# Operand tiles at 0, 32, 64 or 96 bytes into their buffers, and a smaller reserved ring

## The chip, the cores and the metric

One core of a Trainium2 chip runs the whole program. The metric is the device time of one execution in microseconds. The engines named below are TensorE (PE in the rows; PEld is its loading of weights), VectorE (DVE), ScalarE (ACT), GpSimd (POOL) and SyncE (SP), which issues the DMAs.

## What is computed

Two blocks of two layers each on 512 tokens of 1024 features, in float32. What matters of the reference:

```python
# first block, per layer
h = h + 0.5 * (1.0 + gt1) * swiglu(hn, w_ffn1_in[l], w_ffn1_out[l])     # d_ff 2816
mixed = jnp.concatenate([y_att, y_rwkv, y_conv], axis=-1) @ w_mix_out[l]
h = h + (1.0 + gt2) * mixed
h = h + 0.5 * (1.0 + gt3) * swiglu(hn, w_ffn2_in[l], w_ffn2_out[l])
# second block, per layer: the stream x and a context of 256 tokens
out_x, out_c = token_mixers(hx, hc, ...)                                # mLSTM, Fourier, convolution
x = x + mx[2] * rmsnorm(out_x, g_post_mix[l])
x = x + mx[5] * rmsnorm(sq_relu_mlp(hx, w_mlp1[l], w_mlp2[l]), g_post_mlp[l])   # hidden 4096
```

`hn`, `hx` and `hc` are normed and modulated activations. Nearly all of the arithmetic is in the dense products (`@`).

## The kernel before, in words

Activations lie feature-major in SBUF: eight blocks of 128 features, each a tile of 128 partitions by 512 tokens (the context: 256). A dense product takes its weights in panels of 128 output features (128 x 1024 numbers). Both operands are split into a high and a low part in the type float32r, and a product is three passes.

**loadw** (L376) brings one panel by DMA from SP into a raw buffer (two of them), ScalarE casts it to `wh` (L387), VectorE subtracts to give `wl` (L388). There are four buffers for `wh`, four for `wl`, and extra pools where a group of panels has more than four.

**mm3_steps** (L395) is the product of one panel with the eight (or seven, or four) blocks of an operand. For each block it issues three matmuls, and each loads its own 128 x 128 weights:

```python
nc.tensor.matmul(ps, wl[:, s], xh[:, sl], start=k == 0, stop=False)     # L401
nc.tensor.matmul(ps, wh[:, s], xl[:, sl], start=False, stop=False)      # L402
nc.tensor.matmul(ps, wh[:, s], xh[:, sl], start=False, stop=k == n - 1) # L403
```

**sweep** runs panels over segments: the panels in the middle of a phase over all 512 tokens at once, those at its head and tail over halves of 256 tokens, so that the next phase can begin on one half. The operands are `xn` (the normed activations, written by Norm at L275 and L276 or in the opening), `hid` (the hidden panels of an FFN or MLP, written through `split`, L454 and L455), and `xh`/`xl`, `ch`/`cl` and `xr` (mixed outputs, most of them through `split_new`). The order of the work is the program's own; TensorE executes in that order.

**Where the tiles lie.** A pool's buffers follow one another in each partition, each rounded up to 32 bytes. In front stand the reserved ring for dynamic DMAs (16,384 bytes) and four constants (128), then the pool `one`: 544 (onesP), 512 (ident), 8 x 2048 (h), 32, 32, 2496 (cols), 2048 and 1024 (acc). The raw buffers then begin at byte 39,584, which is 309 x 128 + 32. Raw, `wh` and `wl` buffers are 4096 bytes each and the blocks of an operand 2048 (the context: 1024), so that all buffers of a pool have the same remainder modulo 128:

| tiles | first byte | remainder modulo 128 |
|---|---|---|
| `wh`, `wl` (the pools of four) | 47,776 and 64,160 | 32 |
| `xn`, `xh`, `xl`, `xr` of the stream | 92,576 | 32 |
| `hid` of the FFNs (first block) | 128,960 | 64 |
| `wh`, `wl` of the extra pool at the tail of an FFN | 190,400 | 64 |
| `xn`, `ch`, `cl` of the context | 135,648 | 96 |
| `hid` of the MLPs (second block) | 176,608 | 96 |

The slices of a panel for single matmuls are 512 bytes apart, the halves of a block 1024, so a slice has the remainder of its tile.

Of the kernel before, what the change touches and what calls it, by code (L numbers as in the profile page):

```python
"""Two-layer macaron hybrid block followed by a two-layer joint block with a context stream.

Activations live on chip feature-major ([feature, token]); every dense product runs on the tensor
engine in float32r with both operands split exactly into a high and a low part (three passes).
"""
# [8 lines left out]
F32 = mybir.dt.float32  # L14
F32R = mybir.dt.float32r
# [8 lines left out]
T = 512  # L24
# [29 lines left out]
# order of the query heads: block j holds heads j and 4 + j, so that each shares its partitions  # L54
# with the key/value head it attends to
# [18 lines left out]
def _pack(i):  # L74
# [55 lines left out]
    feat = np.r_[2048 + 16:2832, 0:1024, 1024:2048]      # F, C | q, k | v, o  # L130
# [16 lines left out]
def _consts():  # L147
# [5 lines left out]
    c1[:, CI_G1:CI_G1 + 64] = s <= t                     # columns of R  # L153
    c1[:, CI_G1 + 64:CI_G1 + 128] = s < t                # columns of A
# [19 lines left out]
    def dft(n):  # L174
        """cos for frequencies up to n / 2 + 1, then -sin for those below n / 2."""
        j = np.arange(n)
        an = 2 * np.pi * (j[:, None] * j[None] % n) / n
        half = np.concatenate([np.cos(an[:, :n // 2 + 2]), -np.sin(an[:, :n // 2])], axis=1) / math.sqrt(n)
        return np.ascontiguousarray(half.reshape(n // 128, 128, n + 2).astype(f))
# [10 lines left out]

HA, HB = slice(0, 256), slice(256, 512)
OPEN = 5            # panels that go along with the first norm, block by block
GRP = 4             # panels at the head of a phase that go segment by segment
HLAST = 6           # the same in the last MLP
FTAIL = 7           # panels at the tail of an FFN that go segment by segment
MTAIL = 8           # the same of a token mixing
MORE = 3            # temporaries of their own for its tail
DEEP = 2            # hidden panels that go segment by segment with the whole last product of an MLP
DMORE = 3           # temporaries of their own there
PAIR = 4            # squares added up on VectorE  # L200
OFIRST = 3          # output gates ahead of the recurrence
YORD = (6, 7, 0, 1, 2, 3, 4, 5)      # order in which the mixed features become ready
ATT_EVERY = 0.8     # steps per round of what runs side by side
# [5 lines left out]
class MeanSq:  # L209
    """Mean squares over the features of a stream, token-major in PSUM, part by part. The squares of the  # L210
    eight blocks are added up on VectorE, four at a time, and then on the tensor engine (in the one group
    that the zeros open), or on VectorE alone (n: tokens of the stream)."""
# [41 lines left out]
class Norm:  # L254
    """Norm and modulation of a stream, part by part, into split operand tiles."""
# [7 lines left out]
    def __call__(self, acc, sl):  # L263
        k, nc = self.k, self.k.nc
        if self.X is None:
            new = lambda: self.pool.tile([128, self.n], F32R, name="xn", tag=self.tag)
            self.X = [(new(), new()) for _ in range(8)]
# [11 lines left out]
class Kernel:  # L279
    def __init__(self, ctx, tc, a):  # L280
# [4 lines left out]
        self.turn = 0  # L285
# [26 lines left out]
    def temp(self, n, name):  # L312
        """Short-lived [128, n]; half-width ones have buffers of their own."""
        if n > 256:
            return self.tmp.tile([128, T], F32, name=name, tag="nt")[:, :n]
        if self.more is not None and name != "nt":
            return self.more[0].tile([128, 256], F32, name=name, tag=name, bufs=self.more[1])[:, :n]
        return self.tmp.tile([128, 256], F32, name=name, tag="n2", bufs=3)[:, :n]

# [1 line left out]
    def cond_rows(self, pool, i, after=None):  # L321
        """silu of condition i on every partition; not before the tile `after` is there (its use in a
        busy stretch would only delay others)."""
# [10 lines left out]
    def ada_piece(self, pool, src, b0, key, j0, cbs, names):  # L334
        """8 output blocks: one column tile [128, 8] for each conditioning vector in cbs. The work is
        queued in steps; spare() emits them."""
# [16 lines left out]
    def spare(self, n=None):  # L353
        """Emits n queued steps, or all."""
# [20 lines left out]
    def loadw(self, src, pool=None):  # L375
        """src: a weight panel, or several that share a tile."""  # L376
# [8 lines left out]
        wh = (pool or self.whp).tile([128, 1024], F32R, name="wh", tag="wh")  # L385
        wl = (pool or self.wlp).tile([128, 1024], F32R, name="wl", tag="wl")
# [19 lines left out]
    def sweep(self, panels, segs, consume, head=0, tail=0, done=None, extra=None):  # L406
        """panels: weight panels (DRAM); segs: (key, X, slice) in the order in which they become ready.
        The first `head` and the last `tail` panels go segment by segment. consume(panel, key, slice,
        psum); done(key, slice) after a segment's last. extra: room for the weights of groups of over four.
        Narrow panels are loaded in pairs."""  # L410
# [16 lines left out]
        for gi, (ps_, sg) in enumerate(groups):  # L427
# [5 lines left out]
            for key, X, sl in sg:  # L433
                for c in range(0, len(ps_), side):
                    # side by side, block by block as the operand becomes ready
# [21 lines left out]
    def split_new(self, pool, src, tag, n=T, **k):  # L457
        hi = pool.tile([128, n], F32R, name=tag + "h", tag=tag, **k)
        lo = pool.tile([128, n], F32R, name=tag + "l", tag=tag, **k)
# [4 lines left out]
    def scratch(self, name):  # L464
        """Small columns; a phase that runs beside another takes its own."""
# [4 lines left out]
    def rsqrt(self, v):  # L470
        """1/sqrt(v) of v [128, n] (positive): the exponent guess (within 3.5%), a step with fitted
        constants (6.6e-4) and one of third order (1e-9)."""
# [5 lines left out]
        # y holds 3/8 of the root from here on  # L478
# [9 lines left out]
    def stat(self, srcs, sel, n, pp):  # L488
        """Sums over features of srcs * sel: PSUM [128 tokens, tile, w]."""
# [10 lines left out]
    def spread(self, rs, n, w, pp, wp=None, wb=2):  # L500
        """rs [128 tokens, tile, w] -> PSUM [128 features in w groups, n tokens]."""
# [31 lines left out]
    def sigmoid(self, dst, src, bias=0.0):  # L533
        """dst = sigmoid(src + 2 bias) = (1 + tanh(src / 2 + bias)) / 2."""
# [5 lines left out]
    def ffn(self, l, which, norm, gt, nxt, ada=()):  # L540
        """h += 0.5 (1 + gt) swiglu(norm(h)); nxt() gives the norm that follows; norm None: the opening."""
        nc, tc, a = self.nc, self.tc, self.a
        wi, wo = a[f"f{which}i"][l], a[f"f{which}o"][l]
        with ExitStack() as st:
# [7 lines left out]
            for pi, kc in enumerate(pieces):  # L552
                last = pi == len(pieces) - 1
                hid = [tuple(hp.tile([128, T], F32R, name="hid", tag="hid") for _ in range(2)) for _ in range(kc)]
# [43 lines left out]
    def opening(self, hp, adap, panels, up):  # L598
        """The first norm and the first panels, block by block as the input comes in."""
# [3 lines left out]
        with ExitStack() as st:  # L603
# [40 lines left out]
            def block(j):  # L644
# [3 lines left out]
                hi, lo = (self.xp.tile([128, T], F32R, name="xn", tag="x") for _ in range(2))  # L648
# [23 lines left out]
    def attention(self, l, ap, qkv, Z):  # L672
        """A generator. qkv: projected tiles q0-q3, k, v; the outputs, split, go to Z."""
# [12 lines left out]
        # key norm, with the query's gain folded in  # L686
# [6 lines left out]
        # values, token-major  # L693
# [61 lines left out]
        for j in range(4):  # L755
# [3 lines left out]
            # query scales per (token, head): rs * 64 ** -0.5  # L759
# [36 lines left out]
    def shift(self, l, dst, ps, j, sl, last):  # L796
        """Token shift of projected block j out of PSUM; last [128, 1] carries the column before."""
# [11 lines left out]
    def rwkv_group(self, l, rp, P, p, hf):  # L809
        """A pair of heads over half of the tokens; P: shifted projections r0 r1 k0 k1 v0 v1 wdad gd,  # L810
        whose tiles take what comes of them. A generator, so that two pairs can be emitted side by side;
        it returns the output."""
# [16 lines left out]
        # decay and its running sums per chunk  # L829
# [16 lines left out]
        # normalised removal key  # L846
# [20 lines left out]
        # bonus (in v) and gate (in r)  # L867
# [12 lines left out]
        # group norm, bonus, gate  # L880
# [14 lines left out]
    def rwkv_chunks(self, rp, p, RAV, BKB, ep, yp):  # L895
        """Four chunks of 64 tokens for a pair of heads; head 1 has its chunk rows on partitions 64-127."""
# [6 lines left out]
        # for each head and chunk: columns of R, of A, [B K] token-major, [A V] token-major; the rows of  # L903
        # head 1 have their halves the other way round
# [18 lines left out]
        for n in range(6):  # L923
# [17 lines left out]
            if n < 5:  # L941
                # so far nothing lies outside the diagonal blocks of 32
                nc.vector.transpose(Tm.rearrange("p i t -> p (i t)"), TT.rearrange("p i t -> p (i t)"))
            yield
        # M2 V
# [47 lines left out]
    def mesh(parts):  # L993
        """Generators side by side: (generator, its steps per round)."""
# [17 lines left out]
    def mix1(self, l, norm, gt, nxt):  # L1012
# [7 lines left out]
        with ExitStack() as st:  # L1020
# [70 lines left out]
            def rest():  # L1091
                """The rows of w_mix_out of the recurrence and the convolution."""
# [3 lines left out]
                rs = [tuple(self.xp.tile([128, T], F32R, name="xr", tag="x") for _ in range(2)) for _ in range(2)]  # L1096
# [48 lines left out]
    def gates(self, mp, ps, bias, n, m0, gM):  # L1145
        """Running sums and maxima of the gates; rows 0-3 forward, 64-67 backward. A generator that returns them."""
# [25 lines left out]
        gc = mp.tile([128, nt, 4, 4], F32, name=tag, tag=tag)      # g_f, -m_f, g_b, -m_b  # L1172
# [7 lines left out]
    def rows_spread(self, mp, src, name):  # L1180
        """src [128, 1] with rows 0-3 and 64-67 -> [128, 2, 4] on every partition."""
# [34 lines left out]
    def mlstm_head(self, mp, hd, q, k, V1, M, gt, state, sig, gcol, n):  # L1216
        """One head of a stream; sig (sigmoid of the output gate) becomes the mixed output. A generator."""
# [465 lines left out]
```

## Time and profile before

| | before |
|---|---|
| median of 2 runs | 3742.06 us (3741.11 to 3743.01) |
| span of the profiled execution | 3742.2 us |
| TensorE busy | 3674.9 us |
| VectorE busy | 2297.0 us |
| ScalarE busy | 1365.2 us |
| matmuls | 21700 |

A row of the timeline gives the start of an instruction, its duration, its engine, line, operation, the tiles written and read, and shapes. The end of a matmul is modelled, and matmuls overlap in the pipeline: the difference between two starts is the time that one takes of the engine. A row of the groups gives count, busy time and the mean duration of one.

### The profile page before, as it was taken

The page shows a single profiled execution, that of the slowest core. Times are in us where ns is not written, and L with a number is a line of the kernel's source. Part 1 is how long each engine was busy: PE and PEld are TensorE (multiplying, and loading weights), DVE is VectorE, ACT ScalarE, POOL GpSimd, SP SyncE. Part 2 cuts the span into 40 slices and gives each one's busy share as a digit, 9 for nine tenths or more (in the row PEclk, how much of TensorE's full clock was granted, in tenths as well). Part 3 has the DMA queues.
Part 4 walks back from the last instruction along what each step waited for, and adds up shares of the span by engine and source line. Part 5 has one row for each costly group of instructions (what it writes and reads, how often), then busy time and mean ns, then how long its engine had stood idle before and what let it go on. Part 6 is the DMA issues. An engine that isn't in the chain of part 4 may idle for free.

```text
span 3742.2 us, 54388 instructions
## 1 busy us (share of the span) xinstructions
PE 3674.9 (98%) x21700; PEld 3127.7 (84%) x21700; DVE 2297.0 (61%) x4858; ACT 1365.2 (36%) x2505; POOL 5.7 (0%) x42
## 2 busy tenths in 40 slices
PE   8999999999999999999999999999999999999998
PEld 6888877988898889778888888899888897888887
DVE  7565656653356545575778599675644469864334
ACT  3222444422232224443322343455223244354332
POOL 0000000000000000000000000000000000000000
PEclk9999999999999999999999999999999999999999
DMA  7565200263336543111555311123434311132332
GB/s 264 189 208 163 82 29 29 90 215 120 99 97 208 181 138 96 46 36 68 161 191 184 109 53 40 34 81 113 146 113 130 107 36 57 49 94 84 97 96 73
DMA packets 123727, 412.24 MB, mean 110 GB/s; under 512 B 13873, under 2 KB 17713, under 8 KB 123474
## 3 DMA queue, kind: packets, MB, share of 16 engines
q1 hardware_dynamic: 123474, 408.77, 33.8%
q8 instruction: 170, 2.79, 0.3%
q14 instruction: 83, 0.68, 0.1%
HBM read 406.56 MB, written 2.10 MB: 109 GB/s over the span
## 4 chain that ended last, share of the span: by engine, by line
PE 93%; DVE 5%; ACT 1%; DMA 1%; issue 1%; SPq 0%; DVEq 0%; ACTq 0%
PE mm L401 23%; PE mm L402 22%; PE mm L403 22%; PE mc L401 2%; PE mc L403 2%; PE mc L402 2%; PE my L402 2%; PE my L401 2%; PE my L403 2%; PE pn L1268 1%; PE stat L497 1%; PE spr L512 1%; PE sc L712 1%; PE pS L1252 1%; PE po L750 1%
## 5 line engine op out<-in xcount | busy, mean ns | idle before, releaser
L401 PE MATMUL mm<-xn,wl 128*128 128x512 f32 (+1 forms) x2680 | 1011.6, 378 | 3.6 <-DVE rst L483 2.5
L402 PE MATMUL mm<-xn,wh 128*128 128x512 f32 (+1 forms) x2680 | 1004.5, 375 | 0.0
L403 PE MATMUL mm<-xn,wh 128*128 128x512 f32 (+1 forms) x2680 | 1000.0, 373 | 0.0
L388 DVE TENSOR_TENSOR wl<-raw,wh 128x1024 fp32r<-128x1024 f32 (+3 forms) x538 | 636.9, 1185 | 466.1 <-ACT wh L387 464.5
L387 ACT CAST wh<-raw 128x1024 fp32r<-128x1024 f32 (+3 forms) x538 | 546.4, 1017 | 940.2 <-PE mm L403 429.1
L401 PEld LDWEIGHTS mm<-xn,wl 128*128 128x128 f32 x2680 | 507.4, 189 | 97.0 <-issue 12.4
L403 PEld LDWEIGHTS mm<-xn,wh 128*128 128x128 f32 x2680 | 507.2, 189 | 88.0 <-issue 2.1
L402 PEld LDWEIGHTS mm<-xn,wh 128*128 128x128 f32 x2680 | 507.5, 189 | 86.1 <-issue 5.2
L401 PE MATMUL mm<-hid,wl 128*128 128x512 f32 (+1 forms) x1250 | 455.2, 364 | 2.1 <-DVE ox L1587 1.9
L403 PE MATMUL mm<-hid,wh 128*128 128x512 f32 (+1 forms) x1250 | 455.5, 365 | 0.0
L402 PE MATMUL mm<-hid,wh 128*128 128x512 f32 (+1 forms) x1250 | 454.3, 364 | 0.0
L345 DVE CUSTOM_DVE_ANT_0 adaj<-adar,cb 128x1024 bf16<-128x1024 f32 x288 | 351.6, 1221 | 18.5 <-DMA adar<-in_ada_dram 11.0
L401 PEld LDWEIGHTS mm<-hid,wl 128*128 128x128 f32 x1250 | 234.8, 188 | 41.2 <-DVE ox L1587 2.3
L403 PEld LDWEIGHTS mm<-hid,wh 128*128 128x128 f32 x1250 | 234.8, 188 | 40.2
L402 PEld LDWEIGHTS mm<-hid,wh 128*128 128x128 f32 x1250 | 234.7, 188 | 40.1
L565 DVE TENSOR_TENSOR sg<-sg,mm 128x512 f32<-128x512 f32 (+1 forms) x80 | 53.4, 667 | 187.9 <-PE mm L403 182.3
L561 ACT ACTIVATE sg<-mm 128x512 f32<-128x512 f32 (+1 forms) x85 | 49.5, 582 | 301.4 <-PE mm L403 301.4
L402 PE MATMUL mc<-xn,wh 128*128 128x256 f32 x512 | 145.6, 284 | 0.0
L401 PE MATMUL mc<-xn,wl 128*128 128x256 f32 x512 | 145.5, 285 | 0.0
L403 PE MATMUL mc<-xn,wh 128*128 128x256 f32 x512 | 144.6, 283 | 0.0
L401 PE MATMUL mm<-xh,wl 128*128 128x256 f32 x448 | 129.7, 290 | 5.0 <-ACT xh L454 2.9
L402 PE MATMUL mm<-xl,wh 128*128 128x256 f32 x448 | 128.3, 286 | 0.5 <-DVE xl L455 0.5
(432 smaller groups left out, 5325.6 us busy)
## 6 DMA issues: line engine op xcount, KB each, us to landing
adar<-in_ada_dram SPq DMA_DIRECT2D x240, 512.0 KB, 4.5
raw<-in_m_dram SPq DMA_DIRECT2D x96, 512.0 KB, 3.6
raw<-in_f1i_dram SPq DMA_DIRECT2D x88, 512.0 KB, 3.5
raw<-in_f2i_dram SPq DMA_DIRECT2D x88, 512.0 KB, 3.6
raw<-in_w2i_dram SPq DMA_DIRECT2D x46, 512.0 KB, 3.5
raw<-in_mixi_dram SPq DMA_DIRECT2D x40, 512.0 KB, 3.4
raw<-in_m_dram SPq DMA_DIRECT2D x64, 256.0 KB, 3.0
raw<-in_f1o_dram SPq DMA_DIRECT2D x32, 448.0 KB, 3.4
```

The lines of the kernel that those rows point to most:

```text
L345: nc.vector.tensor_tensor_reduce(junk, raw, cb, 1.0, 0.0, ALU.mult, ALU.add, ot[:, j:j + 1])
L387: nc.scalar.copy(wh[:, :n], raw[:, :n])
L388: nc.vector.tensor_sub(wl[:, :n], raw[:, :n], wh[:, :n].bitcast(F32))
L401: nc.tensor.matmul(ps, wl[:, s], xh[:, sl], start=k == 0, stop=False)
L402: nc.tensor.matmul(ps, wh[:, s], xl[:, sl], start=False, stop=False)
L403: nc.tensor.matmul(ps, wh[:, s], xh[:, sl], start=False, stop=k == n - 1)
L497: nc.tensor.matmul(ps[:, j, :], s[:, j * 128:(j + 1) * 128], sel, start=k == 0, stop=k == len(srcs) - 1)
L512: nc.tensor.matmul(ps[:, j * 128:(j + 1) * 128], lhs, self.ident, start=True, stop=True)
L561: nc.scalar.activation(sg, ps, AF.Silu)
L565: nc.vector.tensor_mul(sg, sg, ps)
L712: nc.tensor.matmul(ps[:, i, (0 if qt else 128):], q[rows, qt * 128:(qt + 1) * 128], kn[rows, k0:(qt + 1) * 128], start=True, stop=True)
L750: nc.tensor.matmul(po[rows, qt * 128:(qt + 1) * 128], vt[:, qt - 1 + b, rows], ptt[:, i, b, :], start=n_ == 0, stop=n_ == len(bs) - 1)
```

## The change

Operand tiles get 32 numbers (128 bytes) of room more, and the slice that is used begins 0, 32, 64 or 96 bytes into the buffer. For `xn` and `hid` the place goes by the number of the block, for `wh` and `wl` by a running number of the panel, for `split_new` and `xr` it is always 0. The high and the low part of a block or a panel have the same place. The reserved ring for dynamic DMAs is 1 KB. Comments and docstrings are blanked out, so that lines keep nearly their numbers.

```diff
+PADW = 32
...
-            new = lambda: self.pool.tile([128, self.n], F32R, name="xn", tag=self.tag)
-            self.X = [(new(), new()) for _ in range(8)]
+            new = lambda j: self.k.offset(self.pool, "xn", self.tag, self.n, j)
+            self.X = [(new(j), new(j)) for j in range(8)]
...
-        self.turn = 0
+        self.turn = self.panel = 0
...
+    def offset(self, pool, name, tag, n, j, **k):
+
+        o = 8 * (j % 4)
+        return pool.tile([128, n + PADW], F32R, name=name, tag=tag, **k)[:, o:o + n]
+
...
-        wh = (pool or self.whp).tile([128, 1024], F32R, name="wh", tag="wh")
-        wl = (pool or self.wlp).tile([128, 1024], F32R, name="wl", tag="wl")
+        self.panel += 1
+        wh = self.offset(pool or self.whp, "wh", "wh", 1024, self.panel)
+        wl = self.offset(pool or self.wlp, "wl", "wl", 1024, self.panel)
...
-        hi = pool.tile([128, n], F32R, name=tag + "h", tag=tag, **k)
-        lo = pool.tile([128, n], F32R, name=tag + "l", tag=tag, **k)
+        hi = self.offset(pool, tag + "h", tag, n, 0, **k)
+        lo = self.offset(pool, tag + "l", tag, n, 0, **k)
...
-                hid = [tuple(hp.tile([128, T], F32R, name="hid", tag="hid") for _ in range(2)) for _ in range(kc)]
+                hid = [tuple(self.offset(hp, "hid", "hid", T, j) for _ in range(2)) for j in range(kc)]
...
-                hi, lo = (self.xp.tile([128, T], F32R, name="xn", tag="x") for _ in range(2))
+                hi, lo = (self.offset(self.xp, "xn", "x", T, j) for _ in range(2))
...
-                rs = [tuple(self.xp.tile([128, T], F32R, name="xr", tag="x") for _ in range(2)) for _ in range(2)]
+                rs = [tuple(self.offset(self.xp, "xr", "x", T, 0) for _ in range(2)) for _ in range(2)]
...
-                hid = {k: [tuple(hp.tile([128, n], F32R, name="hid", tag=f"hid{k}") for _ in range(2)) for _ in range(kc)]
+                hid = {k: [tuple(self.offset(hp, "hid", f"hid{k}", n, j) for _ in range(2)) for j in range(kc)]
...
-    nc = _bacc.Bacc("TRN2", target_bir_lowering=False, num_devices=1)
+    nc = _bacc.Bacc("TRN2", target_bir_lowering=False, num_devices=1, dynamic_dma_scratch_size=1024)
```

## Rows read from the trace of the kernel before

**Rows 1.** The page: busy time, share and instructions; granted clock in 40 slices.

```profile
PE 3674.9 (98%) x21700; PEld 3127.7 (84%) x21700; DVE 2297.0 (61%) x4858; ACT 1365.2 (36%) x2505; POOL 5.7 (0%) x42
...
PEclk9999999999999999999999999999999999999999
```

**Rows 2.** The page: the chain that ended last, shares of the span by engine.

```profile
PE 93%; DVE 5%; ACT 1%; DMA 1%; issue 1%; SPq 0%; DVEq 0%; ACTq 0%
```

**Rows 3.** Groups by shape, whole span: count, busy us, mean ns, idle before.

```profile
L401 PE MATMUL mm<-xn,wl 128*128 128x512 f32 x2200 | 874.3, 397 | 0.8 <-ACT yx L1384 0.6 <-ACT sg L561 0.2
...
L401 PE MATMUL mc<-xn,wl 128*128 128x256 f32 x512 | 145.5, 285 | 0.0
...
L401 PE MATMUL mm<-xh,wl 128*128 128x256 f32 x448 | 129.7, 290 | 5.0 <-ACT xh L454 2.9 <-DVE h L1084 1.7 <-DVE wl L388 0.4
```

**Rows 4.** Groups by shape in the first block (0 to 2177 us).

```profile
L401 PE MATMUL mm<-hid,wl 128*128 128x512 f32 x478 | 188.9, 395 | 0.0
```

**Rows 5.** Groups by shape in the second block (2177 us to the end).

```profile
L401 PE MATMUL mm<-hid,wl 128*128 128x512 f32 x448 | 175.2, 391 | 0.0
```

**Rows 6.** Timeline over xn: start us, duration us, instruction; one load of weights.

```profile
999.69 0.39 PE L401 MATMUL mm<-xn,wl 128*128 128x512 f32 x1
...
1000.15 0.19 PEld L401 LDWEIGHTS mm<-xn,wl 128*128 128x128 f32 x1
...
1007.85 0.39 PE L401 MATMUL mm<-xn,wl 128*128 128x512 f32 x1
```

**Rows 7.** Timeline of TensorE over the hid of an FFN, 512 columns.

```profile
839.68 0.40 PE L401 MATMUL mm<-hid,wl 128*128 128x512 f32 x1
...
845.51 0.39 PE L402 MATMUL mm<-hid,wh 128*128 128x512 f32 x1
```

**Rows 8.** Timeline over the MLP's hid: 512 columns, then the context's 256.

```profile
2568.74 0.39 PE L401 MATMUL mm<-hid,wl 128*128 128x512 f32 x1
...
2572.86 0.28 PE L401 MATMUL mc<-hid,wl 128*128 128x256 f32 x1
...
2575.47 0.28 PE L403 MATMUL mc<-hid,wh 128*128 128x256 f32 x1
```

**Rows 9.** Timeline, FFN's hid, 256 columns: extra pool's weights, then the four's.

```profile
1061.79 0.28 PE L401 MATMUL mm<-hid,wl 128*128 128x256 f32 x1
...
1064.43 0.28 PE L402 MATMUL mm<-hid,wh 128*128 128x256 f32 x1
...
1423.81 0.28 PE L403 MATMUL mm<-hid,wh 128*128 128x256 f32 x1
...
1426.61 0.28 PE L403 MATMUL mm<-hid,wh 128*128 128x256 f32 x1
```

**Rows 10.** Timeline behind the switch from an FFN's hid to xn.

```profile
852.98 0.40 PE L401 MATMUL mm<-xn,wl 128*128 128x512 f32 x1
...
853.67 0.40 PE L401 MATMUL mm<-xn,wl 128*128 128x512 f32 x1
...
854.60 0.39 PE L402 MATMUL mm<-xn,wh 128*128 128x512 f32 x1
...
855.96 0.39 PE L402 MATMUL mm<-xn,wh 128*128 128x512 f32 x1
```

**Rows 11.** Timeline behind the switch from xn to an FFN's hid.

```profile
808.17 0.40 PE L401 MATMUL mm<-hid,wl 128*128 128x512 f32 x1
...
808.88 0.40 PE L401 MATMUL mm<-hid,wl 128*128 128x512 f32 x1
...
809.81 0.40 PE L402 MATMUL mm<-hid,wh 128*128 128x512 f32 x1
```

**Rows 12.** Groups by shape: the subtraction that writes a weight panel's low part.

```profile
L388 DVE TENSOR_TENSOR wl<-raw,wh 128x1024 fp32r<-128x1024 f32 x454 | 554.6, 1223 | 406.1 <-ACT wh L387 404.6
```

**Rows 13.** DMA issues: queue, count, KB each, us to landing.

```profile
adar<-in_ada_dram SPq DMA_DIRECT2D x240, 512.0 KB, 4.5
...
crow<-in_cvec_dram SPq DMA_DIRECT2D x1, 4.0 KB
```

## The prediction

> **What bounds the kernel now.** Read the busy line and the clock line first [rows 1]: TensorE is busy for 3674.9 of 3742.2 us, and the granted clock is nine tenths or more, the upper of its two levels (2.4 GHz), in all 40 slices. The chain of work that ended last is 93% TensorE [rows 2]. So the span is the number of matmuls times the time from one matmul's start to the next one's (its pitch); nothing else is near the path. The groups by shape come next [rows 3]: the products are 2200 matmuls of 512 columns over xn on each of the lines 401 to 403 and 478 + 448 over hid [rows 4, 5], 9378 on the three lines, and 2504 of 256 columns a line, some 7500 (nine groups, two of which are shown).
>
> The third view is the timeline, for the pitch. A duration in these rows (0.39 us) is longer than the pitch, because matmuls overlap, so only starts are used. Over xn the starts go from 999.69 to 1007.85 in 36 steps, 226.7 ns each [rows 6]. Over the FFN's hid, with the same shape, the same lines and the same weights' buffers, 839.68 to 845.51 is 25 steps of 233.2 ns [rows 7]. Over the MLP's hid, 2568.74 to 2572.86 is 18 steps of 228.9 ns, and the context's 256 columns behind it take 23 steps of 113.5 ns (2572.86 to 2575.47) [rows 8]. Something other than the shape sets the pitch.
>
> What differs is where the operands lie, by the sums of tile sizes in the section on the kernel. Modulo 128 bytes the weights lie at 32; xn lies at 32 (distance 0), the FFN's hid at 64 (distance 32), the MLP's hid at 96 (distance 64). The strongest pair is one tile with one shape: 256 columns of the FFN's hid take 22 steps of 120.0 ns (1061.79 to 1064.43), where the weights come from the extra pool at 64 (distance 0), and 24 steps of 116.7 ns (1423.81 to 1426.61), where they come from the pool at 32 (distance 32) [rows 9]. The load of the next weights starts with the matmul and lasts 0.19 us of its 0.227 [rows 6], so the two reads run side by side. I take it that they delay each other by an amount that goes by their distance modulo 128.
>
> The trace shows one thing more: the good pitch has to settle. Behind a change of operand the first seven steps are slow even at distance 0: 852.98 to 854.60 is 231.4 ns a step, and only then does it run at 226.7 (854.60 to 855.96, six steps) [rows 10]; from xn to the FFN's hid 808.17 to 809.81 is 234.3 [rows 11]. The first three steps of the two are 0.69 and 0.71 us, 233.3 ns a step in the mean.
>
> **The change, part by part.** *The offsets.* No instruction is added or removed, none is moved past a queue, no wait is added, and the DMAs write the same raw tiles. Weights of a panel go to 32 times (panel mod 4), xn and hid to 32 times (block mod 4). In a product's sum over blocks the weights' place is fixed and the moving operand's steps on by 32 bytes after every three matmuls (lines 401 to 403 of one block). So each matmul over xn or hid, whatever the panel, stands at distance 0, 32, 64 and 96 about a quarter of the time each, and holds a distance for three matmuls, fewer than the seven that settling took. The price is therefore that of the steps right after a change, not that of a settled stretch.
>
> Before, by counts: xn 6600 at 226.7, the FFN's hid 478 x 3 = 1434 at 233.2, the MLP's 448 x 3 = 1344 at 228.9 [rows 3, 4, 5]; the mean is 228.0. Some of these stand behind a switch too; I put 0.5 ns on that (an estimate: about one in ten within seven steps of a switch, 5 ns dearer), 228.5. After: bounds first. Below, the mean of the settled distances 0, 32 and 64, (226.7 + 233.2 + 228.9) / 3 = 229.6, 96 left out since no operand lies there; above, the dearest stretch behind a switch, 234.3. The steps of 3 are nearest to what the change makes, 233.3; since the fourth distance is unknown, and the seven-step means are 231.4 and 234.3, I take 232.5. That is +4.0 ns x 9378 = +37.5 us; with the bounds +10 and +54 us.
>
> *The 256 columns.* Distance 0 settles at 120.0, 32 at 116.7, 64 at 113.5 [rows 8, 9]; mixed, between 113.5 and 120, and I take 117.5, against about 118 before (xn and xh of the first block lie at distance 0, the context at 64). The tiles of split_new keep offset 0, so that their distance goes by the panel alone. Some 7500 x -0.5 = -4 us, with bounds of -15 and +15 us (2 ns either way).
>
> *The engines that write the tiles.* The subtraction of a weight panel on VectorE (1.22 us [rows 12]) and the cast on ScalarE before it write to another offset; I cost that at nothing, below and above, because TensorE's 24 matmuls on a panel take 24 x 0.227 = 5.4 us and hide them. Without that cover one tenth more on 454 subtractions would be 454 x 0.12 = 55 us.
>
> *The ring.* 15,360 bytes fewer in front of everything is 120 x 128, so no remainder changes. All 28 listed kinds of DMA are issued by SP, from adar to crow, and half a megabyte lands in 4.5 us [rows 13]; POOL is busy for 5.7 us in all [rows 1]. I cost it at nothing; if landing doubled to 9 us, it would pass the 5.4 us of a panel, and two raw buffers would still cover a part of that.
>
> The sum: 3742.2 + 37.5 - 4 = 3776 us. The profiled span is 0.14 us over the median of the runs (3742.06), so it needs no correction.
>
> **A rule of the Trainium skill speaks against this.** The rows say 226.7 and 233.2 ns for one shape [rows 6, 7]. In "SBUF — State Buffer", section "A bandwidth-pool intuition that's wrong (but worth ruling out)", the skill gives TensorE a second, independent read port for its weight loads; by that the place of an operand costs nothing. The trace disagrees as far as 116.7 against 120.0 on one tile goes [rows 9]. "TensorE: Matmul & The Clock Gate", section "Back-to-back issue gap", has 512 / 2.4 + 2.5 = 216 ns for one matmul of 512 columns; if every one took that, the time would be an estimated 3742 - 9378 x 12.5 ns = 3625 us, and no row here shows such a pitch.
>
> **The rivals.**
> (1) *Places don't matter.* The three pitches belong to the phases (other writers, other PSUM buffers), not to the addresses. For it: xn and hid come in different phases, and distance is read from the layout, not from the trace. Against it: one tile with two pitches [rows 9]. Then the time is 3742.
> (2) *Mixing is cheap, the kernel gets faster.* The place is the same products; the mechanism is a fourth distance at which the two reads pass each other, or a cycle of twelve matmuls that settles low. For it: 113.5 ns exists for 256 columns [rows 8], 6.5 under the dearest. Against it: no steady stretch of 512 columns is under 226.7. With 512 columns at 226.7 (-1.8 x 9378 = -17 us) and 256 at 115 (-3 x 7500 = -22 us) the time is 3703. With that gain on 256 columns it decides below 228.5 + 22 / 9.378 = 230.8 ns for 512 columns; for 2% (75 us) the 512 columns would have to fall to some 223 as well.
> (3) *Every matmul pays the dearest price.* Distances change so often that each step is the first behind a switch (0.71 us for three, 236.7 [rows 11]) and 256 columns stay at 120: +8.2 x 9378 = 77 us and +2 x 7500 = 15 us, 3834 us. Against it: 231.4 behind the switch in [rows 10].
> (4) *The ring is used after all*, and weights come late. Against it: no issue on POOL [rows 13]. If each of the 454 full panels [rows 12] came 0.1 us late, 45 us: 3787.
>
> **How the numbers follow.** The forecast 0.69, with a range of its own of 3750 to 3800 (lower and upper bounds above, the 256 columns added in part). Rival 1 0.08, rival 2 0.16 (the fourth distance is not seen), rival 3 0.05, rival 4 0.02. A measurement of this kernel tells 2% from no change, 75 us. Faster by that only in a corner of rival 2, 0.03; slower in rival 3, 0.05; within 2% 0.92. The range 3715 to 3800 holds the forecast but for its edges, rivals 1 and 4 and the upper half of rival 2: 0.8.
>
> **What would show it.** Right: steps over xn between 231 and 235 ns with no settled 226.7 anywhere, steps over the FFN's hid a little under 233.2, the same instruction counts, and TensorE still busy for 98%. Wrong in the price: distance 96 with a pitch under 226 or over 236 in the twelve-step pattern. Wrong in the mechanism: steps of 226.7 over xn as before (rival 1). Rival 4 would show as TensorE waiting for wl or wh.

## The result, and the profile after

The changed kernel takes 3771.43 us (median of 2 runs, 3770.46 to 3772.39) against 3742.06: a ratio of 1.0076, with a 95% interval of 1.0047 to 1.0106. It is slower by 29 us: clear of the noise, but less than 2%. The profiled execution has a span of 3768.7 us, 26.5 more than before.

The page's busy line, clock line and chain, to be read against [rows 1, 2]:

```profile
PE 3703.9 (98%) x21700; PEld 3128.2 (83%) x21700; DVE 2296.7 (61%) x4858; ACT 1366.2 (36%) x2505; POOL 5.7 (0%) x42
...
PEclk9999999999999999999999999999999999999999
...
PE 92%; DVE 6%; ACT 1%; issue 1%; DMA 1%; SPq 0%; DVEq 0%; ACTq 0%
```

TensorE is busy for 29.0 us longer with the same 21,700 instructions, and the granted clock is nine tenths or more in all 40 slices as before (mean 0.987 before, 0.988 after); VectorE, ScalarE and GpSimd stand where they were. TensorE's idle time went from 67.3 to 64.8 us, which gives 2.5 us of it back.

The groups by shape, which answer [rows 3, 4, 5] (count, busy us, mean ns; the lines are seven further down). The two rows on `hid` are one view over the first block and one over the second:

```profile
L408 PE MATMUL mm<-xn,wl 128*128 128x512 f32 x2200 | 882.8, 401 | 0.8 <-ACT yx L1391 0.5 <-ACT sg L568 0.2
...
L408 PE MATMUL mc<-xn,wl 128*128 128x256 f32 x512 | 145.8, 285 | 0.0
```

```profile
L408 PE MATMUL mm<-hid,wl 128*128 128x512 f32 x478 | 188.5, 394 | 0.0
...
L408 PE MATMUL mm<-hid,wl 128*128 128x512 f32 x448 | 176.7, 394 | 0.0
```

Over xn the mean duration rose from 397 to 401 ns, over the FFN's hid it fell from 395 to 394, over the MLP's hid it rose from 391 to 394: the three operands have moved together. The timeline has the pitch. Three stretches, over xn, the FFN's hid and the MLP's hid, each by its first start and the first start behind it (to be read against [rows 6, 7, 8]):

```profile
163.02 0.40 PE L408 MATMUL mm<-xn,wl 128*128 128x512 f32 x1
...
240.85 0.39 PE L408 MATMUL mm<-hid,wl 128*128 128x512 f32 x1
...
814.26 0.39 PE L408 MATMUL mm<-hid,wl 128*128 128x512 f32 x1
...
858.71 0.39 PE L408 MATMUL mm<-xn,wl 128*128 128x512 f32 x1
...
3439.61 0.40 PE L408 MATMUL mm<-hid,wl 128*128 128x512 f32 x1
...
3484.12 0.39 PE L408 MATMUL mm<-xn,wl 128*128 128x512 f32 x1
```

They have 336, 192 and 192 steps: 231.6, 231.5 and 231.8 ns each, where they were 226.7, 233.2 and 228.9. Over the whole trace, taking every step between two product matmuls without a wait, the mean pitch of 512 columns went from 228.6 to 231.66 ns (9243 steps, +28.3 us) and that of 256 columns from 117.98 to 118.14 (7128 steps, +1.1 us). That is all of TensorE's 29 us.

Nothing came late elsewhere. The weight subtraction takes as long as in [rows 12], the half megabyte of `adar` lands in 4.8 us against 4.5 [rows 13], and the waits of TensorE by releaser (total us, times, longest) have no weight panel but one of 0.4 us, which before had too:

```profile
L395 DVE TENSOR_TENSOR wl<-raw,wh 128x1024 fp32r<-128x1024 f32 x454 | 554.8, 1223 | 416.3 <-ACT wh L394 414.9
```

```profile
adar<-in_ada_dram SPq DMA_DIRECT2D x240, 512.0 KB, 4.8
```

```profile
PE stat L504 <- DVE acc L231: 9.6, 4, 7.7
PE spr L519 <- DVE rsy L492: 7.0, 8, 3.9
...
PE mm L408 <- DVE wl L395: 0.4, 1, 0.4
```

### The profile page after: what moved, and what is told of

It reads as the page before. It is cut to its first block, busy times and chain, and to the rows that moved or that the text cites. A ratio compares the mean times of both kernels' runs of the same rounds, so it can differ in the third digit from the quotient of the medians.

```text
span 3768.7 us, 54391 instructions
## 1 busy us (share of the span) xinstructions
PE 3703.9 (98%) x21700; PEld 3128.2 (83%) x21700; DVE 2296.7 (61%) x4858; ACT 1366.2 (36%) x2505; POOL 5.7 (0%) x42
## 4 chain that ended last, share of the span: by engine, by line
PE 92%; DVE 6%; ACT 1%; issue 1%; DMA 1%; SPq 0%; DVEq 0%; ACTq 0%
PE mm L408 23%; PE mm L409 22%; PE mm L410 22%; PE mc L408 2%; PE mc L410 2%; PE mc L409 2%; PE my L409 2%; PE my L408 2%; PE my L410 2%; PE pn L1275 1%; PE stat L504 1%; PE spr L519 1%; PE sc L719 1%; PE pS L1259 1%; PE po L757 1%
## 5 line engine op out<-in xcount | busy, mean ns | idle before, releaser
L409 PE MATMUL mm<-xn,wh 128*128 128x512 f32 (+1 forms) x2680 | 1009.8, 377 | 0.0
L409 PEld LDWEIGHTS mm<-xn,wh 128*128 128x128 f32 x2680 | 506.4, 189 | 94.8 <-issue 5.2
L409 PE MATMUL mm<-hid,wh 128*128 128x512 f32 (+1 forms) x1250 | 454.5, 364 | 0.0
L410 PEld LDWEIGHTS mm<-hid,wh 128*128 128x128 f32 x1250 | 234.7, 188 | 41.5
L408 PEld LDWEIGHTS mm<-hid,wl 128*128 128x128 f32 x1250 | 234.7, 188 | 41.3 <-DVE ox L1594 2.3
L409 PEld LDWEIGHTS mm<-hid,wh 128*128 128x128 f32 x1250 | 234.9, 188 | 39.9
L409 PE MATMUL mc<-xn,wh 128*128 128x256 f32 x512 | 146.0, 285 | 0.0
L409 PE MATMUL mm<-xl,wh 128*128 128x256 f32 x448 | 127.8, 285 | 0.5 <-DVE xl L462 0.5
```

## The experiments

"Mean pitch" below is always that of all steps without a wait, as above. The kernel before has 228.60 ns for 512 columns and 117.98 for 256.

**The ring alone (e1_ring).** The kernel before with

```diff
+    nc = _bacc.Bacc("TRN2", target_bir_lowering=False, num_devices=1, dynamic_dma_scratch_size=1024)
```

> The kernel before with the 1 KB ring alone; no offsets, no room. Theory (the pitch goes by the distance of the two operands modulo 128 bytes, and the ring moves everything by 120 x 128): no change, 3740 to 3745 us, xn at 226.7 ns a step. Rival (the smaller ring slows the DMAs): the whole of the loss, 3765 to 3775 us, with TensorE waiting for wh or wl.

Measured: 3743.81 us against 3744.68, a ratio of 0.9993 (0.9984 to 1.0003); mean pitch 228.60 and 118.00 ns. The ring costs nothing.

**The room without the places (e2_pad).** The changed kernel, in `offset`:

```diff
-        o = 8 * (j % 4)
+        o = 0
```

> The changed kernel with every offset set to 0: the 128 bytes of room behind each operand buffer and the 1 KB ring stay. Theory: all remainders are those of before, so 3740 to 3745 us, with settled steps of 226.7 ns over xn, 233.2 over the hid of the FFNs and 228.9 over that of the MLPs. Rival (buffers 2176 or 4224 bytes apart instead of 2048 and 4096 are what costs): 3765 to 3775 us.

Measured: 3767.71 us, ratio 1.0059 (1.0044 to 1.0074), span 3765.3; mean pitch 231.29 and 118.10 ns. So 2.7 of the 3.1 ns come with the 128 bytes of room, with no tile at another place in its buffer. By my distance modulo 128 nothing should have moved: the expectation failed, and the time lies in its rival's range. The reason is in the sizes: before, the high and the low tile of a block were 2048 bytes apart; now it is 2176, and neighbouring weight buffers are 4224 apart. Modulo 256 that is 128 each time. The timeline shows what follows. Over xn, three starts 24 matmuls apart, two panels in a row:

```profile
163.27 0.40 PE L408 MATMUL mm<-xn,wl 128*128 128x512 f32 x1
...
168.77 0.40 PE L408 MATMUL mm<-xn,wl 128*128 128x512 f32 x1
...
174.38 0.39 PE L408 MATMUL mm<-xn,wl 128*128 128x512 f32 x1
```

The first panel, whose weights by the layout lie 128 from the high and 0 from the low parts, has 5.50 / 24 = 229.2 ns a step; the second, with the two exchanged, 5.61 / 24 = 233.8. That made modulo 256 the next theory.

**One half of the places each (e3_weights, e4_blocks).** Only the weights step, or only the blocks:

```diff
+        o = 8 * (j % 4) if tag == "wh" or tag == "wl" else 0     # e3_weights
+        o = 0 if tag == "wh" or tag == "wl" else 8 * (j % 4)     # e4_blocks
```

> Weights step on by 32 bytes from panel to panel, the blocks of xn and hid all stay at 0. A distance now holds for the 24 matmuls of a panel. Theory (settled pitch by distance, plus some seven steps to settle behind a switch): over xn a quarter each of 226.7, 233.2, 228.9 and an unknown one, in the mean 230 to 231 ns with the settling, so +14 to +23 us, 3756 to 3765 us, and inside a panel the steps visibly come to rest. Rival (any mixture costs the same, settling plays no part): 3771 us as changed.

> Only the blocks of xn and hid step on by 32 bytes, all weights stay at 0. The distance changes after every three matmuls as in the changed kernel. Theory: only the distance counts, so the same as changed, 3767 to 3775 us and 231 to 232 ns a step of 512 columns. Rival (the weights' own place has a part in it): 3742 to 3760 us.

Measured: e3_weights 3775.95 us, ratio 1.0084 (1.0068 to 1.0101), mean pitch 232.31 and 117.98; e4_blocks 3771.99 us, ratio 1.0071 (1.0056 to 1.0086), 231.72 and 118.30. e4_blocks came as expected. e3_weights missed its 3756 to 3765 us and is above its rival's 3771 too: with 128 bytes of room a distance does not hold for the 24 matmuls of a panel, as that expectation had it; by the layout it still changes by 128 before and behind the middle one of each three. Either half adds 0.4 to 1.0 ns to e2_pad's 231.29, and both together 0.4: they don't add up, and the room stays the larger part. That the place of the moving operand alone does not decide, e3_weights shows against e2_pad: only weights were moved, and the steps over xn went from 231.15 to 232.59 ns.

**Room of 256 bytes, places at 0 (e5_pad256).**

```diff
-PADW = 32
+PADW = 64
-        o = 8 * (j % 4)
+        o = 0
```

> Room of 256 bytes behind each operand buffer instead of 128, every offset 0, ring 1 KB. After the run with 128 bytes of room alone cost nearly the whole loss, the theory is changed: the distance counts modulo 256 bytes, and room of 128 bytes makes the high and the low part of a block, which are neighbours, lie 128 bytes apart, so that the distance changes with every matmul. Theory: 256 bytes leave all distances as before, 3740 to 3745 us, 226.7 ns a step over xn. Rival (buffers that do not follow each other at a multiple of 2048 bytes cost as such): 3764 to 3771 us.

Measured: 3743.55 us against 3743.91, ratio 0.9999 (0.9990 to 1.0008); mean pitch 228.62 and 117.99. Over the FFN's hid and then over xn, 192 and 336 steps:

```profile
117.76 0.40 PE L408 MATMUL mm<-hid,wl 128*128 128x512 f32 x1
...
162.56 0.40 PE L408 MATMUL mm<-xn,wl 128*128 128x512 f32 x1
...
238.76 0.40 PE L408 MATMUL mm<-hid,wl 128*128 128x512 f32 x1
```

233.3 and 226.8 ns: the pitches of [rows 6, 7] are back, although nearly every tile lies elsewhere. Room in itself costs nothing; what counts is the distance of moving operand and weights modulo 256 bytes.

**The places with 256 bytes of room (e6_off256).** The changed kernel with `PADW = 64`; high and low parts then have one distance, which holds for three matmuls, as the prediction had taken it.

> The changed kernel with 256 bytes of room instead of 128: high and low part now have the same place modulo 256, and the distance holds for the three matmuls of a block, as the prediction had taken it for the changed kernel. Theory (settling takes about seven matmuls): still unsettled, 231 to 233 ns a step of 512 columns, 3765 to 3778 us. Rival (the alternation of high and low part by 128 bytes was the whole loss, three matmuls are enough to settle): a mean of settled distances, 3742 to 3757 us.

Measured: 3777.75 us, ratio 1.0097 (1.0080 to 1.0114), span 3775.9; mean pitch 232.24 and 118.20. Over xn, 336 steps of 232.1:

```profile
163.37 0.40 PE L408 MATMUL mm<-xn,wl 128*128 128x512 f32 x1
...
241.36 0.39 PE L408 MATMUL mm<-hid,wl 128*128 128x512 f32 x1
```

This is the pattern that the prediction had worked out (232.5 ns, 3776 us), except that by the layout it runs through eight distances modulo 256 and not four; it comes within 0.3 ns.

**One distance per phase (e7_scan, e8_fine, e9_scan3).** With 256 bytes of room, weights at place 0 and a fixed place for all blocks of a phase (in numbers of 4 bytes; the distance is four times that, for hid 32 more in the first block and 64 more in the second, for the context 64 more):

```diff
+XO = [0, 32, 8, 16, 40, 24, 48, 56, 24, 32]     # xn, in turn; other lists in the other two
+HO = [0, 24, 32, 40, 48, 48, 8]                 # hid
...
+        o = self.place(tag)
```

> 256 bytes of room; all weights at offset 0; each normed operand and each hid has one place for its whole life, another one in each phase. Distances modulo 256, in order of the program: xn of the first FFN 0, first mixing 128, second FFN 32, third FFN 64, second mixing 160, fourth FFN 96, mixing of the second block 192, its MLP 224, second mixing 96, second MLP 128; hid of the four FFNs 128, 160, 192, 224, of the two MLPs 0 and 96; the context's 192. Theory: one settled pitch for each distance, the same for xn and hid: 0 226.7, 32 233.2, 64 228.9 ns, the others unknown. Rival (the pitch goes by phase and tile): xn 226.7 everywhere, FFN hid 233.2, MLP hid 228.9.

> As the scan of distances, with small ones: xn 4, 8, 16, 48, 24, 12, 28, 20, 112, 80 in the order of the phases, hid of the FFNs 4, 8, 16, 24, of the MLPs 12 and 28, the context's 16 bytes. Theory with lines of 32 bytes: the pitch lies between that of distance 0 (226.7) and of 32 (233.2) for 4 to 28, and moves in small steps. Rival (only whole multiples of 32 or 64 count): 226.7 for all of 4 to 28. Open: whether any distance is cheaper than 226.7.

> A further scan of distances modulo 256, one for each operand of each phase: xn 36, 40, 52, 60, 76, 92, 104, 120, 144, 252 in the order of the phases, hid of the FFNs 228, 244, 220, 124, of the MLPs 44 and 56, the context's 112. Theory (settled pitch is a function of the distance alone): each distance has one pitch of 512 columns between 226.7 and 237 ns, as all sixteen so far. Open: whether one is under 226.7, as no distance has been so far.

Measured, one execution each: 3774.5, 3769.5 and 3772.2 us. The phases are the result. From e7_scan, xn at distances 0, 32 and 64, and hid at 128 (first and last start; 335 steps each, for hid 191):

```profile
162.16 0.39 PE L422 MATMUL mm<-xn,wl 128*128 128x512 f32 x1
...
238.11 0.39 PE L424 MATMUL mm<-xn,wh 128*128 128x512 f32 x1
...
858.05 0.39 PE L422 MATMUL mm<-xn,wl 128*128 128x512 f32 x1
...
936.22 0.39 PE L424 MATMUL my<-xn,wh 128*128 128x512 f32 x1
...
1230.30 0.39 PE L422 MATMUL mm<-xn,wl 128*128 128x512 f32 x1
...
1306.98 0.39 PE L424 MATMUL my<-xn,wh 128*128 128x512 f32 x1
...
117.37 0.40 PE L422 MATMUL mm<-hid,wl 128*128 128x512 f32 x1
...
161.93 0.39 PE L424 MATMUL my<-hid,wh 128*128 128x512 f32 x1
```

226.7, 233.3, 228.9 and 233.3 ns. The same operand in the same kind of phase takes the pitch that its distance had in the kernel before: the theory of e7_scan came true, and its rival, the phase, is out. From e8_fine, xn at distance 4 (335 steps) and hid at 28 (191):

```profile
165.62 0.40 PE L422 MATMUL mm<-xn,wl 128*128 128x512 f32 x1
...
244.91 0.40 PE L424 MATMUL mm<-xn,wh 128*128 128x512 f32 x1
...
3442.39 0.39 PE L422 MATMUL mm<-hid,wl 128*128 128x512 f32 x1
...
3485.69 0.39 PE L424 MATMUL mm<-hid,wh 128*128 128x512 f32 x1
```

236.7 and 226.7. Neither expectation of e8_fine came true: 4 bytes cost more than 32, and 28 bytes no more than 0. From e9_scan3, hid at 244 (191 steps), the dearest of all at 512 columns, 240.0, above the expected 237:

```profile
818.38 0.40 PE L422 MATMUL mm<-hid,wl 128*128 128x512 f32 x1
...
864.22 0.40 PE L424 MATMUL mm<-hid,wh 128*128 128x512 f32 x1
```

The theory of e9_scan3, one pitch for each distance, fails as well. Two stretches over the same xn tiles at distance 92 (first and last start, 335 steps each):

```profile
1929.11 0.39 PE L422 MATMUL mm<-xn,wl 128*128 128x512 f32 x1
...
2007.27 0.40 PE L424 MATMUL mm<-xn,wh 128*128 128x512 f32 x1
...
2046.14 0.39 PE L422 MATMUL mm<-xn,wl 128*128 128x512 f32 x1
...
2123.75 0.39 PE L424 MATMUL my<-xn,wh 128*128 128x512 f32 x1
```

233.3 and 231.7 ns, each steady from its first steps to its last. So at some distances there is more than one pitch that lasts, and which of them a stretch takes, the distance does not say. Distances 36 (236.7 or 234.7) and 48 (233.3 or 230.0) are like that too; at 0, 28, 32, 60, 64 and 252 all long stretches of 512 columns agree.

**Cheap distances in turn (e11_cheap4).** How much is the mixture of dear distances, and how much the switching? Here the blocks step through the four distances that settle at 226.67:

```diff
+FOUR4 = (0, 28, 60, 252)
...
+        base = 0 if tag == "x" else 64 if tag == "c" else 32 if self.hi <= 4 else 64
+        return (FOUR4[j % 4] - base) % 256 // 4
```

> All weight tiles lie at one remainder modulo 256 bytes; the blocks of xn and hid step in turn through the four distances behind them that settled at 226.67 ns with 512 columns in the scans: 0, 28, 60 and 252 bytes (with 256 columns 120, 115.6, 116.7 and 116.7 ns). 256 bytes of room per tile, ring of 1 KB; what is computed is that of before. So the distance changes as often as in the changed kernel, but no distance is a dear one. Theory that a switch of distance is itself paid for, with several steps to settle as in [rows 10, 11]: mean of 512 columns 229 to 231 ns against 226.7 without a switch, 3740 to 3765 us. Rival, that the time is the mean of the settled pitches and a switch costs nothing: 512 columns 226.7 to 227.0 ns (228.6 before, so about -18 us over 9612), 256 columns 117.2 to 117.5 (118.0 before, -5 us over 7512), 3715 to 3725 us.

Measured: 3749.2 us against 3743.44, ratio 1.0012 (1.0002 to 1.0022), span 3751.6; mean pitch 229.59 and 117.72. Over xn, 336 steps of 229.4:

```profile
163.39 0.39 PE L416 MATMUL mm<-xn,wl 128*128 128x512 f32 x1
...
240.48 0.39 PE L416 MATMUL mm<-hid,wl 128*128 128x512 f32 x1
```

A switch after every three matmuls costs 2.9 ns a step of 512 columns even where each of the distances is a cheap one: the theory that a switch is paid for stands, the mean of settled pitches falls.

**Everything at distance 28 (e10_all28).** One distance that is cheap for both shapes, with no switch inside a product or between xn and hid; the weights of the extra pools are moved to the others' remainder (126 matmuls of 256 columns at the tail of the first FFN miss it, by the layout, in e11_cheap4 too):

```diff
+XO = [7, 7, 7, 7, 7, 7, 7, 7, 7, 7]
+HO = [0, 63, 63, 63, 63, 55, 55]
+CO = 55
+WO = {"w6": 32, "ep1": 56, "ep": 48, "ep2": 48, "ep3": 48}
```

> All normed operands, mixed outputs and hid lie 28 bytes behind the weights modulo 256, the weights of the extra pools are put at the remainder of the pools of four, 256 bytes of room, ring 1 KB. Theory (distance 28 settles at 226.7 ns for 512 columns and at 115.5 for 256, as the scan has them): 512 columns from 228.6 to 227.0, 9612 x -1.6 = -15 us, 256 columns from 118.0 to 115.8, 7512 x -2.2 = -17 us, so 3705 to 3716 us. Rival (the short pitch needs the surroundings that it was seen in): between 3735 and 3772 us.

Measured: 3713.97 us against 3744.94, ratio 0.9921 (0.9908 to 0.9935), span 3710.2; mean pitch 226.71 and 115.63. The busy line, and xn over 335 steps of 226.7:

```profile
PE 3641.3 (98%) x21700; PEld 3104.3 (84%) x21700; DVE 2294.9 (62%) x4858; ACT 1365.6 (37%) x2505; POOL 5.7 (0%) x42
```

```profile
160.81 0.39 PE L423 MATMUL mm<-xn,wl 128*128 128x512 f32 x1
...
236.75 0.39 PE L425 MATMUL mm<-xn,wh 128*128 128x512 f32 x1
```

It came as expected, and beats the kernel before by 31 us and the changed one by some 57. By steps, 512 columns gave 9245 x 1.89 = 17.5 us and 256 columns 7124 x 2.35 = 16.7 us; the span gained 32.0.

## Why the prediction was right or wrong

**The bound was right, and the kind of mechanism.** TensorE's pitch went by where the operands lie, not by the phase, and a switch of distance is paid for (e11_cheap4). Over xn 231.6 ns without a settled 226.7, over the FFN's hid a little under 233.2, instruction counts as before, TensorE at 98%: as the prediction had listed. Rival 1, 3742 us, is out by the timeline and by the interval. The second read port that the Trainium skill gives the weight loads ("SBUF — State Buffer", section "A bandwidth-pool intuition that's wrong (but worth ruling out)") does not make places free here: 226.7 and 233.3 ns in e7_scan differ by the place alone.

**The step that failed is "modulo 128".** The rows had operands at distances 0, 32 and 64, and these have the same remainder modulo 128 and modulo 256, so they could not tell the two apart; I chose the smaller. From it came "each matmul stands at distance 0, 32, 64 and 96 ... and holds a distance for three matmuls". In truth the 128 bytes of room alone put the middle one of each three matmuls (L409, on the low part) 128 bytes off the other two, the distances are eight and not four, and the switch comes within three matmuls. e2_pad shows it: 231.29 ns with no places at all. The prediction had looked for the loss in the places and gave the room no cost, while 23.1 of the 26.5 us of span come with the room (by the medians 23 of 29 us).

**The term of 512 columns was over-sized, in the main for that reason**: 232.5 ns predicted, 231.66 measured; +37.5 us in the sum, +28.3 in the trace. With the distance held as the prediction took it (e6_off256) the pitch is 232.24 and the median 3777.75 us, so 232.5 was close to the price of the wrong pattern, though it was picked between 229.6 and 234.3 and not derived. That the pattern which really runs costs nearly the same was luck: nothing in the prediction says so, and at the 229.2 ns of e2_pad's first panel its forecast would have been some 31 us too high. Two smaller items: the 0.5 ns added for switches before was right (228.0 settled, 228.6 measured), and the 9378 matmuls of 512 columns leave out 234 that write `my` (9612 in all), worth 1 us.

**Why about 232 in either pattern.** Two parts, each seen by itself. The mixture: by the scan the eight distances that are multiples of 32 settle at 232.05 ns in the mean ((226.7 + 228.9 + 5 x 233.3 + 234.3) / 8). The switching: e11_cheap4 has 229.6 where 226.7 would be settled. How long a switch is felt is not fixed: from distance 32 to 0 it was seven steps [rows 10], from 128 to 0 three (e7_scan, behind 162.16 us). They don't simply add: e6_off256 has 232.24 where its own distances settle at 231.2 in the mean, but the changed kernel's 231.66 is under the 232.05 of its settled pitches. In e2_pad the first panel has 229.2 with two of three matmuls at a distance that settles at 233.3 (231.1 in the mean), the second 233.8 with one of three (228.9). A repeating pattern of distances has a pitch of its own, which I can measure but not work out; that stays open.

**The term of 256 columns was wrong in sign, within its bounds**: -4 us predicted, +1.1 measured. Steps over xn fell from 118.75 to 118.18, as expected of leaving distance 0, but those over hid rose from 116.44 to 118.18: the MLP context's 113.5 [rows 8] went when the distances were mixed. I had counted it as the price of distance 64 and as an end that a mixture may reach. It isn't even the only price of that distance: in the trace of before the context's xn, also at 64, runs settled at 117.8 ns (682 steps), and hid in part at 113.5 and in part at 117.8. One short stretch was too little to set a price on.

**The items costed at nothing were right**: the ring (e1_ring, 0.9993), the writers (1223 ns before and after), the waits. Rival 4 has no trace of its wait on weights. Rival 3 needed 236.7 ns and 120.0; neither came. Rival 2 is refuted as it stood, since no mixture ran under 229 ns as a mean (e11_cheap4's 229.59 is the lowest), but it had named 226.7 and 115 ns as what could be had: e10_all28 reaches 226.71 and 115.63, with one distance instead of a cycle.

## What to carry to other kernels

Where TensorE sets the span and starts follow one another without a wait, look at start-to-start times of one shape over different operands: a difference of a few ns with the same shape and clock can be the byte distance of moving operand and weights. Padding or staggering tiles moves that distance for everything behind it, so a room that isn't a multiple of 256 bytes is an edit in itself. Choose one good distance and hold it, rather than rotate places; here that was worth 0.8%, and rotation among four that are equally good at 512 columns lost what they had to give.

## What the runs showed of the hardware

Settled pitch in ns by distance modulo 256 bytes (address of the moving tile less that of the weights), float32r with 128 x 128 weights, from the three scans; behind each switch some ten steps are left out, and where stretches differ both paces are given. For 512 columns these are all the distances that were tried, for 256 a part of them:

| columns | distance: pitch |
|---|---|
| 512 | 0: 226.7; 4: 236.7; 8: 233.3; 12: 228.9; 16: 231.7; 20: 235.9; 24: 233.3; 28: 226.7; 32: 233.3; 36: 234.7 or 236.7; 40: 233.3; 44: 230.0; 48: 230.0 or 233.3; 52: 233.3; 56: 230.0; 60: 226.7; 64: 228.9; 76: 228.4; 80: 231.1; 92: 231.7 or 233.3; 96: 233.3; 104: 232.7 and 112: 230.4 (means of short stretches); 120: 234.2; 124: 230.0; 128: 233.3; 144: 233.3; 160: 234.3; 192: 233.3; 220: 230.0; 224: 233.3; 228: 236.7; 244: 240.0; 252: 226.7 |
| 256 | 0: 120.0; 4: 123.3; 8: 116.7, 120.0 or 126.7; 12: 116.7; 28: 115.6; 60: 116.7; 64: 113.3 (kernel before) or 117.8; 96: 120.0; 104: 120.0 or 130.0; 112: 113.3 to 115.6; 128: 118.7; 192: 113.3 or 117.8; 244: 122.2; 252: 116.7 |

Four things in it I had not expected. Four bytes matter (226.7 at 0, 236.7 at 4), so it is not a matter of whole 32-byte lines. No distance goes below 226.67 ns for 512 columns, and four reach it exactly (0, 28, 60, 252), with steps that repeat within 1 ns in the scans, while elsewhere single steps can range more widely (229 to 238 at 128, 229 to 243 at 228). And the best distance for 512 columns is not that for 256: 0 is the floor for the one and dear for the other. The difference between best and worst is 5.9% for 512 columns and 14.7% for 256, where the 130.0 is one stretch of 46 settled steps (e9_scan3, over xh at 2471 us). With either width one distance can have two paces (36, 48 and 92 for 512 columns; 8, 64, 104 and 192 for 256), so the distance isn't all of it. Why these distances and not others, and what chooses between two paces, the runs don't show, and whether the same table holds for other types was not tried.
